# Spatial products over four banks, weights in another order, and a third adaLN chunk on VectorE

## The chip, the cores and the metric

The kernel runs on one core of a Trainium2 chip. The metric is the device time of one execution in microseconds (us). A core has TensorE (PE; its weight loads are listed apart as PEld), VectorE (DVE), ScalarE (ACT), GpSimd (POOL) and SyncE (SP), which issues the transfers here. Each takes its own instructions in order; semaphores hold them to each other. The weights and tokens lie in HBM and come through 16 DMA engines. TensorE writes to PSUM, which has eight banks of 512 fp32 values per partition.

## The reference, cut to what matters

Two layers over 512 latent and 256 context tokens of width 1024. Each layer normalises the tokens, scales and shifts them by adaLN terms (`silu(c) @ ada_w + ada_b`, split into shift, scale and gate), mixes them, and adds the gated result. Layer 0 mixes by a gated MLP (A, the place of this change) and differential attention (B); layer 1 by latent attention. Branch A:

```
u, v, z = xl @ w_in[:, :512], xl @ w_in[:, 512:1024], xl @ w_in[:, 1024:1536]
u, v = gelu(u), layer_norm(gelu(v))
mixed[p, g] = sum_q w_s[g, p, q] * v[q, g] + b_s[g, p]     # 8 groups, chunks of 128 tokens
a = u * mixed * silu(z)
```

## The kernel before

All products of fp32 operands are done in three matmuls (`mm3`, L79 to L81): each operand is split into a high part `h` (ScalarE, L66) and a low part `l` (VectorE, L67), and h·h, h·l and l·h are added up in PSUM. A weight is loaded into a `raw` buffer (two of them), split, and used.

**Order of work.** The program is traced in the order of the Python code, and a planner then sets each engine's order from priorities (the traced order), free buffers and its own estimate of times. `in_order(...)`, `issue_after(...)` and `add_manual_dep(..., NO_SYNC)` force an order on one engine where it is wanted.

**Start.** The tokens are squared and summed (`ssq_quarter` on ACT, `ssq_vector` on DVE), `rstd_of` (L266 on) gives 1/rms of the four latent tiles, and later of the two context tiles; `normalise` (L395) scales the tokens, PE turns them (`turned`, L402), and `modulate_in` (L405 on) makes the high part on ACT (L414) and, on DVE, `xm` (L416) and the low part (L421). All this stands within `in_order(ACT, DVE, PE)` for the first quarter of the width (L455 on).

**The gated MLP** (L542 to L574) comes after the products of v (`av_part`), whose layer norm runs on DVE and ACT meanwhile.
- Two projections for u (`b` = 0, 1), each of three pairs of token tiles, 48 matmuls of 256 columns a pair (`proj_tok`). When a pair is done, `ev` takes it out with a Gelu (L548).
- Eight spatial groups (L557 on): three matmuls of 384 columns into a bank of `ps_mm`, which has two, and one DVE instruction (L563) that adds the bias and multiplies by u.
- Two projections for z, taken out with a Silu (L568) into `z` (two buffers) and multiplied in on DVE (L572).

**adaLN chunks.** What the two layers need of `silu(c) @ ada_w` is cut into 12 chunks. Chunks go two ways. On PE (`ada_step`, called from `ev`): four transfers of 512 KB, then `ada_products` (L175), one copy, and in the next `ev` a transpose (`ada_rows`, L188). On DVE (`ada_piece`): a chunk is four pieces; a piece is one transfer of 512 KB (L236) and two multiplications with a running sum (L246), one for the latent and one for the context vector. Four chunks go over PE here (`ada_rest`), the layer 1 chunks 2 and 3 over DVE, as eight pieces. Both share the seven buffers `ada`; `pieces_ahead(n)` asks for the next n loads. The first piece may run once the layer norm is done (`normed`), the rest after the last spatial instruction.

**Queues around it.** All loads are on SP's queue, in the order that the planner gives them; a load that waits for a buffer holds up the loads behind it. The spatial weights `wsT` go into the shared pool `wp`, the weights of the z projections into the eight buffers `wo` (four weights with two parts each).

Of the kernel before, what the change touches and what calls it, by code (L numbers as in the profile page):

```python
# [18 lines left out]
P = 128  # L19
# [11 lines left out]
def tile_backbone(ctx: ExitStack, tc: tile.TileContext, a: dict, out: bass.AP):  # L31
# [71 lines left out]
    def fill(pl, tag, n):  # L103
        pl.tile([P, n], F32, tag=tag, name=tag)

    gsum = cst.tile([P, 8], F32, name="gsum")
    asum = cst.tile([P, 2, 4, 2], F32, name="asum")
    fill(cst, "fill0", 72)
    ident = cst.tile([P, P], F32, name="ident")
    cvec = const("cvec", [P, 8, 2])  # L110
    fill(cst, "fill1", 64)
# [55 lines left out]
    def shift_of(li, kt, v):  # L167
        return AD[:, li, kt // 2, kt % 2, v:v + 1]
# [37 lines left out]
        ada_rows(li, j, ada_products(ws, between))  # L206


    ada_rest = [(0, 4), (0, 5), (1, 0), (1, 1)]
    ada_loaded = []  # L210

    def ada_ahead():
# [26 lines left out]
    def ada_piece(after):  # L239

        k = len(pieces_done)
        w = pieces[k]
        j, b = divmod(k, 4)
        for v in range(2):
            jk = w if v else til(p_a, [P, D], F32, "lnwb")
            i = DVE.scalar_tensor_tensor(jk, w, 1.0, csb[v], op0=ALU.mult, op1=ALU.mult, accum_out=asum[:, j, b, v:v + 1])  # L246
            tc.add_manual_dep(i.ins, after.ins.name, NO_SYNC, reason="in_order")
        pieces_done.append(k)
        if b == 3:
            ada_bias(1, 2 + j, asum[:, j])  # L250

    def gate_rows(g, li, v):

# [148 lines left out]
            PE.transpose(ps[:, t * P:(t + 1) * P], xq[j][:, t0 + t, i * P:(i + 1) * P], ident)  # L402
        return ps[:, :n * P]

    def modulate_in(j, v, i, xh, xl, ps=None, between=None):  # L405

        t0, n = ((0, 4), (4, 2))[v]
        cols = slice(t0 * P, (t0 + n) * P)
        kt = 2 * j + i
        if ps is None:  # L410
            ps = turned(j, v, i, tr_ps())
        m = til(p_in, [P, NL], F32, "xm", 2)[:, :n * P]
        g = gT[:, 0, kt, v:v + 1]
        h = ACT.activation(xh[:, i, cols], ps, AF.Identity, bias=shift_of(0, kt, v), scale=g)  # L414
        if v == 0:
            DVE.tensor_scalar(m, ps, g, shift_of(0, kt, v), op0=ALU.mult, op1=ALU.add)  # L416
        else:
            ACT.activation(m, ps, AF.Identity, bias=shift_of(0, kt, v), scale=g)
        if between:
            between()  # L420
        DVE.tensor_tensor(xl[:, i, cols], m, xh[:, i, cols].bitcast(F32), op=ALU.subtract)  # L421
        return h


# [37 lines left out]
    with in_order(ACT, DVE, PE):  # L462
        normalise(0, 0)
        xt0 = []

        def fill_in(kt):
            if kt < 5:
                turn_over(2)
            else:
                i = len(xt0)  # L470
                xt0.append(turned(0, 0, i, tr_ps() if i else avb[4]))
        ada_chunk(0, 0, adaw[0], between=fill_in)
        ACT.activation(w0h, w0, AF.Copy)
        turn_over(6)
        modulate_in(0, 0, 0, *XT[0], ps=xt0[0],
                    between=lambda: DVE.tensor_tensor(w0l, w0, w0h.bitcast(F32), op=ALU.subtract))
        for q in range(1, 4):
            ssq_vector(q, 5)
        modulate_in(0, 0, 1, *XT[0], ps=xt0[1])
        for q in range(4):  # L480
            ssq_quarter(xq[q], acc, q, 4, 1 if q else 2)
        rs.append(rstd_of(acc, 4, 2))
        normalise(1, 0)
        h = normalise(0, 1)
    ws_in = [(w0h, w0l)]
# [57 lines left out]
    ada_ahead()  # L543

    au = [til(p_mix, [P, 6, 256], F32, "au", 2) for _ in range(2)]
    for b in range(2):
        def ev(p, ps, b=b):
            ACT.activation(au[b][:, 2 * p:2 * p + 2, :], ps, AF.Gelu)  # L548
            if b and p == 1:
                ada_piece(normed)  # L550
            ada_step()
            if b:
                pieces_ahead((4, 2, 2)[p])
        proj_tok(XT, load_w256(wch[4 + 2 * b:6 + 2 * b], *((p_a, 8) if b else ())), range(3), ev)

    wsh, wsl = (x.rearrange("p (g n) -> p g n", g=8) for x in load_w(a["wsT"]))
    for g in range(8):  # L557
        ps = mm_ps()
        o = ps[:, :384].rearrange("p (t n) -> p t n", t=6)
        s = (slice(None), slice(None), slice(g * 64, (g + 1) * 64))  # L560
        mm3(o, (wsh[:, g, :], wsl[:, g, :]), (vnh[s], vnl[s]), True, True)
        u = au[g // 4][:, :, (g % 4) * 64:(g % 4 + 1) * 64]
        last = [DVE.scalar_tensor_tensor(u, o, absT[:, g:g + 1], u, op0=ALU.add, op1=ALU.mult)]  # L563

    for b in range(2):
        def ev(p, ps, b=b):
            z = sp.tile([P, 2, 256], F32, tag="z", name=nm("z"))
            ACT.activation(z, ps, AF.Silu)  # L568
            ada_step()
            for _ in range(1 if b + p else 2):  # L570
                ada_piece(last[-1])
            i = DVE.tensor_tensor(au[b][:, 2 * p:2 * p + 2, :], au[b][:, 2 * p:2 * p + 2, :], z, op=ALU.mult)  # L572
            last.append(i)
        proj_tok(XT, load_w256(wch[8 + 2 * b:10 + 2 * b], p_a, 8), range(3), ev)  # L574


    p_a.release()
# [451 lines left out]
    silu2(csl, load_raw(a["crow"][0]))  # L1029

    def gate_step(b, after):
        w = load_raw(a["adr"][8 + b])
        i = DVE.scalar_tensor_tensor(w, w, 0.5, csl, op0=ALU.mult, op1=ALU.mult, accum_out=gsum[:, b:b + 1])
        tc.add_manual_dep(i.ins, after.name, NO_SYNC, reason="in_order")
        if b == 7:
            DVE.tensor_tensor(AD[:, 1, 4:, :, 0], gsum.rearrange("p (j b) -> p j b", j=2), adab[:, 1, 4:, :], op=ALU.add)
# [99 lines left out]
def _layout(i):  # L1136
    A = {k: np.asarray(v) for k, v in i.items()}
    r = {}
    x = np.concatenate([A["x"][0], A["ctx"][0]], 0)
    r["x"] = x.reshape(6, P, 4, 256).transpose(2, 1, 0, 3)  # L1140
    c = np.stack([A["c"][0], A["c_ctx"]], 0)
    r["cvec"] = c.reshape(2, 8, P).transpose(2, 1, 0)
    r["normw"] = A["norm_w"].reshape(2, 8, P).transpose(2, 0, 1)
    ada, adab = [], []
    for li in range(2):
        W = A["ada_w"][li].T
        for j in range(6):
            if j < 4:
                rows = np.r_[j * 256:(j + 1) * 256, D + j * 256:D + (j + 1) * 256]
            else:  # L1150
                rows = np.arange(2 * D + (j - 4) * 512, 2 * D + (j - 3) * 512)
            ada.append(W[rows].reshape(4, P, D))
            adab.append(A["ada_b"][li][rows])
    r["ada"] = np.stack([w.reshape(512, 4, 2, P).transpose(1, 3, 2, 0).reshape(4, P, 1024) for w in ada])
    r["adr"] = np.concatenate(ada[8:12])
    r["crow"] = np.broadcast_to(c[:, None], (2, P, D))
    r["adab"] = np.stack(adab).reshape(2, 6, 4, P).transpose(3, 0, 1, 2)
    r["cos"], r["sin"] = _rope_tables()
    r["absT"] = A["a_bs"][0].T
    r["subw"] = A["b_subln_w"][0][:, None]  # L1160
    lqk = np.stack([A["b_lq1"][0], A["b_lk1"][0], A["b_lq2"][0], A["b_lk2"][0]])
    r["lqk"] = np.broadcast_to(lqk, (P, 4, 64))
    r["lnwb"] = np.broadcast_to(np.stack([A["a_ln_w"][0], A["a_ln_b"][0]]), (P, 2, 512))
    w = A["even_w_in"][0]
    au, av, az = w[:, :512], w[:, 512:1024], w[:, 1024:1536]
    bq, bk, bv, bz = w[:, 1536:2048], w[:, 2048:2560], w[:, 2560:3072], w[:, 3072:]
    qk = np.stack([_chunks(bq, 128, 8), _chunks(bk, 128, 8)], 1).reshape(8, P, 1024)
    r["ew"] = np.concatenate([_chunks(av, 512, 2), _chunks(au, 256, 4), _chunks(az, 256, 4), _chunks(bv, 256, 4),
                              qk, _chunks(bz, 128, 8)])
    r["wsT"] = A["a_ws"][0].transpose(2, 0, 1).reshape(P, 1024)  # L1170
    r["ewo"] = _chunks(A["even_w_out"][0], 256, 4)
    o = A["odd_w_in"][0]
    owa = o[:, :448].reshape(8, P, 448).transpose(1, 0, 2)
    r["owa"] = owa.reshape(P, 4, 896).transpose(1, 0, 2)
    r["owz"] = _chunks(o[:, 448:], 128, 8)
    wq = A["c_wq_b"][0].reshape(256, 8, 192)
    r["wqT"] = wq[:, :, :128].transpose(2, 1, 0).reshape(P, 2, 1024).transpose(1, 0, 2)
    r["wqr"] = wq[:, :, 128:].reshape(2, P, 512).transpose(1, 0, 2).reshape(P, 1024)
    wkv = A["c_wkv_b"][0].reshape(128, 8, 256)
    r["wkT"] = wkv[:, :, :128].transpose(2, 1, 0).reshape(P, 1024)  # L1180
    r["wv"] = wkv[:, :, 128:].reshape(P, 1024)
    r["cqw"] = A["c_q_norm_w"][0].reshape(2, P).T
    r["ckw"] = A["c_kv_norm_w"][0][:, None]
    r["owo"] = _chunks(A["odd_w_out"][0], 256, 4)
    r["finw"] = np.broadcast_to(A["final_w"], (P, D))
    return {k: np.ascontiguousarray(v, dtype=np.float32) for k, v in r.items()}
# [14 lines left out]
```

## Time and profile before

| | |
|---|---|
| median of 3 runs | 697.11 us (697.02 to 700.86) |
| profiled execution | 698.24 us; its span 696.5 us, so 1.7 us lie around the span |
| granted clock over the span | 0.996 |
| busy share of the span | PE 98%, PEld 90%, DVE 67%, ACT 52%, POOL 3% |
| chain that ended last | PE 77%, DVE 4%, ACT 2%, DMA 1% |

A busy PE says that matmuls are in flight, not that they follow each other at full pace; so the starts of the matmuls are read too. A row of a timeline gives start, duration, engine, line, operation, output and inputs, shape, how many were merged, and in brackets the idle time of the engine before it and what ended it.

### The profile page before, as it was taken

Reading aid. Unit: us, or ns where it says so; the run is one execution under the profiler, and the core shown is the slowest. Engines: PE = TensorE matmul, PEld = TensorE weight load, DVE = VectorE, ACT = ScalarE, POOL = GpSimd, SP = SyncE. Lnnn points to the kernel's source line nnn. Section 1 sums busy time; section 2 is a strip of 40 time slices with the busy share of each in tenths; the row PEclk is TensorE's granted clock in tenths of the full one; section 3 lists DMA queues with packets and bytes.
Section 4 is the critical chain, followed back from the end, with each engine's and each line's share of the span. In section 5 each row is a group of like instructions: output and inputs, shape, how many; then the busy total and the mean of one; then the engine's idle time right before and its main releaser. Section 6 shows DMA issues by size and latency. Waiting matters only on the chain.

```text
span 696.5 us, 12408 instructions
## 1 busy us (share of the span) xinstructions
PE 682.5 (98%) x5118; PEld 628.9 (90%) x5118; DVE 468.5 (67%) x867; ACT 364.5 (52%) x706; POOL 20.3 (3%) x27
## 2 busy tenths in 40 slices
PE   8999998999999999999999999999999999999995
PEld 8678997999998899899899999988889999999995
DVE  2647738646597965979675428766458898876764
ACT  5856324115475754766534314444358787886432
POOL 1000000010001000010000000010000000000000
PEclk9999999999999999999999999999999999999998
DMA  8965894101100011000613300250210212110402
GB/s 339 408 230 224 310 372 155 31 1 61 62 31 31 1 61 61 32 30 1 242 61 119 111 1 10 65 198 31 92 61 9 83 62 62 32 61 31 121 32 92
DMA packets 20361, 69.93 MB, mean 100 GB/s; under 512 B 3152, under 2 KB 3280, under 8 KB 20304
## 3 DMA queue, kind: packets, MB, share of 16 engines
q1 hardware_dynamic: 20304, 69.13, 28.2%
q8 instruction: 40, 0.66, 0.4%
q14 instruction: 17, 0.14, 0.1%
HBM read 67.02 MB, written 2.10 MB: 99 GB/s over the span
## 4 chain that ended last, share of the span: by engine, by line
PE 77%; DVE 4%; ACT 2%; DMA 1%; issue 0%; SPq 0%; POOLq 0%; ACTq 0%
PE mm L79 17%; PE mm L81 17%; PE mm L80 17%; PE S L80 3%; PE S L81 3%; PE S L79 3%; PE tr L1005 3%; PE S L644 2%; PE S L646 2%; PE tr L662 2%; PE S L983 1%; PE S L987 1%; DMA wr<-in_ew 1%; PE tr L79 1%; PE tr L679 1%; PE tr L293 1%
## 5 line engine op out<-in xcount | busy, mean ns | idle before, releaser
L80 PE MATMUL mm<-xl,wh 128*128 128x512 f32 (+1 forms) x240 | 84.6, 352 | 0.0
L81 PE MATMUL mm<-xh,wl 128*128 128x512 f32 (+1 forms) x240 | 84.5, 352 | 0.0
L79 PE MATMUL mm<-xh,wh 128*128 128x512 f32 (+1 forms) x240 | 84.2, 351 | 0.0
L67 DVE TENSOR_TENSOR wl<-wr,wh 128x1024 fp32r<-128x1024 f32 (+1 forms) x40 | 48.3, 1209 | 41.2 <-ACT wh L66 39.6
L369 ACT ACTIVATE e<-S,s 128x768 f32<-128x768 f32 (+1 forms) x80 | 65.3, 817 | 17.4 <-DVE s L368 16.7
L368 DVE TENSOR_REDUCE s<-S 128x1 f32<-128x768 f32 (+1 forms) x80 | 67.2, 842 | 3.7 <-PE S L987 1.8
L66 ACT ACTIVATE wh<-wr 128x1024 fp32r<-128x1024 f32 (+1 forms) x40 | 41.8, 1048 | 50.9 <-PE mm L80 21.3
L66 ACT ACTIVATE ah<-tr 128x512 fp32r<-128x512 f32 x76 | 43.9, 596 | 24.8 <-PE tr L662 12.6
L67 DVE TENSOR_TENSOR al<-tr,ah 128x512 fp32r<-128x512 f32 x76 | 50.3, 685 | 7.6 <-ACT ah L66 6.7
L79 PEld LDWEIGHTS mm<-xh,wh 128*128 128x128 f32 x240 | 45.2, 188 | 5.1 <-ACT wh L66 0.2
L79 PE MATMUL mm<-wh,xh 128*128 128x256 f32 (+1 forms) x172 | 49.7, 289 | 0.0
L80 PEld LDWEIGHTS mm<-xl,wh 128*128 128x128 f32 x240 | 45.1, 188 | 5.0
L80 PE MATMUL mm<-wl,xh 128*128 128x256 f32 (+1 forms) x172 | 49.6, 288 | 0.0
L81 PEld LDWEIGHTS mm<-xh,wl 128*128 128x128 f32 x240 | 45.2, 188 | 4.8
L81 PE MATMUL mm<-wh,xl 128*128 128x256 f32 (+1 forms) x172 | 49.0, 287 | 0.0
L79 PE MATMUL mm<-wo,xh 128*128 128x256 f32 x144 | 40.7, 283 | 0.9 <-DVE au L563 0.9
L81 PE MATMUL mm<-wo,xl 128*128 128x256 f32 x144 | 40.3, 280 | 0.0
L80 PE MATMUL mm<-wo,xh 128*128 128x256 f32 x144 | 40.3, 280 | 0.0
L79 PEld LDWEIGHTS mm<-wh,xh 128*128 128x128 f32 x172 | 32.5, 189 | 1.1 <-ACT xh L414 0.3
L156 POOL TENSOR_TENSOR s<-s,mhalf 128x6 f32<-128x6 f32 (+4 forms) x15 | 16.0, 1071 | 585.6 <-DVE s L1107 225.1
L80 PEld LDWEIGHTS mm<-wl,xh 128*128 128x128 f32 x172 | 32.4, 188 | 0.4
L81 PEld LDWEIGHTS mm<-wh,xl 128*128 128x128 f32 x172 | 32.3, 188 | 0.5
(330 smaller groups left out, 2000.6 us busy)
## 6 DMA issues: line engine op xcount, KB each, us to landing
ada<-in_ada SPq DMA_DIRECT2D x32, 512.0 KB, 7.8
wr<-in_ew SPq DMA_DIRECT2D x28, 512.0 KB, 3.5
ada<-in_adr SPq DMA_DIRECT2D x8, 512.0 KB, 6.6
wr<-in_ewo SPq DMA_DIRECT2D x8, 512.0 KB, 3.4
wr<-in_owz SPq DMA_DIRECT2D x8, 512.0 KB, 3.6
wr<-in_adr SPq DMA_DIRECT2D x8, 512.0 KB, 3.4
wr<-in_owo SPq DMA_DIRECT2D x8, 512.0 KB, 3.9
xr<-in_x SPq DMA_DIRECT2D x4, 768.0 KB, 6.3
```

The source lines that it names most:

```text
L66: ACT.activation(h, src, AF.Copy)
L67: (eng or DVE).tensor_tensor(l, src, h.bitcast(F32), op=ALU.subtract)
L79: PE.matmul(ps, lh, rh, start=first, stop=False)
L80: PE.matmul(ps, lh, rl, start=False, stop=False)
L81: PE.matmul(ps, ll, rh, start=False, stop=last)
L156: return POOL.tensor_tensor(dst, src, mhalf[:, :n], op=ALU.pow)
L368: mx = DVE.tensor_reduce(nmx[:, :1], v[:, :, :w], axis=AX.XY, op=ALU.max, negate=True)
L369: ACT.activation(e.rearrange("p (c k) -> p c k", k=w), v[:, :, :w], AF.Exp, bias=nmx[:, :1], scale=1.0, accum_out=sm[:, col:col + 1])
L644: PE.matmul(S[:, c, :n], QS[:, m, qs], KS[:, m, k0:k0 + n], start=True, stop=False)
L646: scored = PE.matmul(S[:, c, :n], QS[:, m, qs], KL[:, m, k0:k0 + n], start=False, stop=True)
L662: PE.transpose(ps[:, i * 256 + q * P:i * 256 + (q + 1) * P], es[q][:, (2 * j + i) * P:(2 * j + i + 1) * P], ident)
L1005: PE.transpose(ps[:, i * 256 + q * P:i * 256 + (q + 1) * P], es[q][:, (2 * j + i) * P:(2 * j + i + 1) * P], ident)
```

## The change

- The spatial products go by turns into `ps_mm` and into the first half of a tile of `ps_s`: four banks rather than two.
- Chunk (1, 1) leaves `ada_rest` and becomes four more pieces on DVE; the running sums are one chunk larger, the layout of the piece weights starts one chunk earlier. Pieces are spread anew: 2 before the spatial instructions (1 before), then 2, 2, 2, 2, 1, 1 over the six pairs of the z projections (2, 1, 1, 1, 1, 1 before). Loads of pieces are asked for from the last pair of the first u projection on.
- Weights: `wsT` and those of the first z projection are traced ahead of the second u projection; those of the second z projection keep their place, but their ACT part is put behind the last Gelu, their DVE part behind the last spatial instruction.
- At the start, `xm` and the low part of the second turned tile come after `rstd_of` of the context tiles on DVE, instead of before.

```
-    asum = cst.tile([P, 2, 4, 2], F32, name="asum")
-    fill(cst, "fill0", 72)
+    asum = cst.tile([P, 3, 4, 2], F32, name="asum")
+    fill(cst, "fill0", 64)
...
-    ada_rest = [(0, 4), (0, 5), (1, 0), (1, 1)]
+    ada_rest = [(0, 4), (0, 5), (1, 0)]
...
-            ada_bias(1, 2 + j, asum[:, j])
+            ada_bias(1, 1 + j, asum[:, j])
...
-    def modulate_in(j, v, i, xh, xl, ps=None, between=None):
+    def modulate_in(j, v, i, xh, xl, ps=None, between=None, only=None):
...
         h = ACT.activation(xh[:, i, cols], ps, AF.Identity, bias=shift_of(0, kt, v), scale=g)
-        if v == 0:
-            DVE.tensor_scalar(m, ps, g, shift_of(0, kt, v), op0=ALU.mult, op1=ALU.add)
-        else:
-            ACT.activation(m, ps, AF.Identity, bias=shift_of(0, kt, v), scale=g)
-        if between:
-            between()
-        DVE.tensor_tensor(xl[:, i, cols], m, xh[:, i, cols].bitcast(F32), op=ALU.subtract)
+
+        def low():
+            if v == 0:
+                DVE.tensor_scalar(m, ps, g, shift_of(0, kt, v), op0=ALU.mult, op1=ALU.add)
+            else:
+                ACT.activation(m, ps, AF.Identity, bias=shift_of(0, kt, v), scale=g)
+            if between:
+                between()
+            DVE.tensor_tensor(xl[:, i, cols], m, xh[:, i, cols].bitcast(F32), op=ALU.subtract)
+        if only == "h":
+            return low
+        low()
         return h
...
-        modulate_in(0, 0, 1, *XT[0], ps=xt0[1])
+        second = modulate_in(0, 0, 1, *XT[0], ps=xt0[1], only="h")
         for q in range(4):
             ssq_quarter(xq[q], acc, q, 4, 1 if q else 2)
         rs.append(rstd_of(acc, 4, 2))
+        second()
         normalise(1, 0)
...
+    w_az, behind = [], {}
     for b in range(2):
         def ev(p, ps, b=b):
-            ACT.activation(au[b][:, 2 * p:2 * p + 2, :], ps, AF.Gelu)
-            if b and p == 1:
+            gelu = ACT.activation(au[b][:, 2 * p:2 * p + 2, :], ps, AF.Gelu)
+            behind[ACT.engine] = gelu.ins.name
+            if b and p < 2:
                 ada_piece(normed)
             ada_step()
-            if b:
-                pieces_ahead((4, 2, 2)[p])
-        proj_tok(XT, load_w256(wch[4 + 2 * b:6 + 2 * b], *((p_a, 8) if b else ())), range(3), ev)
-
-    wsh, wsl = (x.rearrange("p (g n) -> p g n", g=8) for x in load_w(a["wsT"]))
+            if b or p == 2:
+                pieces_ahead((4, 3, 2, 3)[3 * b + p - 2])
+        w = load_w256(wch[4 + 2 * b:6 + 2 * b], *((p_a, 8) if b else ()))
+        if b:
+            wsh, wsl = (x.rearrange("p (g n) -> p g n", g=8) for x in load_w(a["wsT"]))
+            w_az.append(load_w256(wch[8:10], p_a, 8))
+        proj_tok(XT, w, range(3), ev)
+
     for g in range(8):
-        ps = mm_ps()
+        ps = ps_s.tile([P, 2, 512], F32, tag="S", name=nm("S"))[:, 0, :] if g % 2 else mm_ps()
...
+    behind[DVE.engine] = last[-1].ins.name
     for b in range(2):
         def ev(p, ps, b=b):
...
             ada_step()
-            for _ in range(1 if b + p else 2):
+            for _ in range(2 if 3 * b + p < 4 else 1):
                 ada_piece(last[-1])
...
-        proj_tok(XT, load_w256(wch[8 + 2 * b:10 + 2 * b], p_a, 8), range(3), ev)
+        if b:
+
+            n = len(nc.cur_bb.bb.instructions)
+            w_az.append(load_w256(wch[10:12], p_a, 8))
+            for i in nc.cur_bb.bb.instructions[n:]:
+                if i.engine in behind:
+                    tc.add_manual_dep(i, behind[i.engine], NO_SYNC, reason="in_order")
+        proj_tok(XT, w_az[b], range(3), ev)
...
-        w = load_raw(a["adr"][8 + b])
+        w = load_raw(a["adr"][12 + b])
...
-    r["adr"] = np.concatenate(ada[8:12])
+    r["adr"] = np.concatenate(ada[7:12])
```

## Rows read from the trace of the kernel before

**Rows 1.** The page, engines: busy us, share of the span, instructions.
```profile
PE 682.5 (98%) x5118; PEld 628.9 (90%) x5118; DVE 468.5 (67%) x867; ACT 364.5 (52%) x706; POOL 20.3 (3%) x27
```
**Rows 2.** Windows: length, then busy us (instructions) by engine, granted clock, DMA share, GB/s.
```profile
105.00:115.00 10.00, 7.28 (x41) 5.54 (x41) 7.58 (x11) 4.17 (x5) 0.00 (x0) 1.00 0.44 141
115.00:130.00 15.00, 15.00 (x129) 15.00 (x129) 13.41 (x23) 3.97 (x5) 0.00 (x0) 1.00 0.32 107
130.00:150.00 20.00, 20.00 (x167) 19.78 (x167) 10.18 (x21) 2.39 (x4) 2.94 (x4) 1.00 0.00 1
```
**Rows 3.** Timeline of PE over the spatial products (L79 to L81).
```profile
106.60 0.34 PE L79 MATMUL mm<-vnh,wh 128*128 128x384 f32 x1
...
106.95 0.33 PE L81 MATMUL mm<-vnh,wl 128*128 128x384 f32 x1
107.56 0.44 PE L79 MATMUL mm<-vnh,wh 128*128 128x384 f32 x1 [0.28 <-ACT au L548]
...
108.87 0.44 PE L79 MATMUL mm<-vnh,wh 128*128 128x384 f32 x1 [0.52 <-DVE au L563]
...
111.05 0.45 PE L79 MATMUL mm<-vnh,wh 128*128 128x384 f32 x1 [0.86 <-DVE au L563]
...
112.56 0.44 PE L79 MATMUL mm<-vnh,wh 128*128 128x384 f32 x1 [0.19 <-DVE au L563]
...
114.75 0.39 PE L79 MATMUL mm<-wo,xh 128*128 128x256 f32 x1 [0.87 <-DVE au L563]
```
**Rows 4.** Timeline of DVE over the same stretch.
```profile
107.06 1.23 DVE L67 TENSOR_TENSOR wo<-wr,wo 128x1024 fp32r<-128x1024 f32 x1 [5.49 <-ACT wo L66]
108.20 1.14 DVE L563 SCALAR_TENSOR_TENSOR au<-mm,absT_sb,au 128x384 f32<-128x384 f32 x2
109.25 1.22 DVE L67 TENSOR_TENSOR wo<-wr,wo 128x1024 fp32r<-128x1024 f32 x1
...
112.94 1.22 DVE L67 TENSOR_TENSOR wl<-wr,wh 128x1024 fp32r<-128x1024 f32 x1
114.08 1.14 DVE L563 SCALAR_TENSOR_TENSOR au<-mm,absT_sb,au 128x384 f32<-128x384 f32 x2
```
**Rows 5.** Timeline of ACT at the end of the u projections.
```profile
105.97 1.06 ACT L66 ACTIVATE wo<-wr 128x1024 fp32r<-128x1024 f32 x1 [4.33 <-DMA wr<-in_ew]
106.93 0.58 ACT L548 ACTIVATE au<-mm 128x512 f32<-128x512 f32 x1
```
**Rows 6.** Timeline of PE around the fourth chunk (L175) and the transpose after it (L188).
```profile
93.18 0.27 PE L188 MATMUL tr<-ident,arow 128*128 128x128 f32 x1
93.39 1.96 PE L175 MATMUL tr<-ada,c 128*32 128x128 f32 x64
95.27 0.38 PE L79 MATMUL mm<-wo,xh 128*128 128x256 f32 x1
...
100.84 0.27 PE L188 MATMUL tr<-ident,arow 128*128 128x128 f32 x1
```
**Rows 7.** Timeline of ACT, one Silu of the z projections.
```profile
132.02 0.60 ACT L568 ACTIVATE z<-mm 128x512 f32<-128x512 f32 x1 [5.05 <-PE mm L81]
```
**Rows 8.** Timeline of all engines at the start, around the context tiles' 1/rms.
```profile
20.61 0.81 DVE L416 TENSOR_SCALAR xm<-tr,gT,AD 128x512 f32<-128x512 f32 x1
...
22.06 0.15 DVE L268 TENSOR_REDUCE s<-s 128x2 f32<-128x8 f32 x1
...
22.20 0.30 PEld L457 LDWEIGHTS mm<-wh,xl 128*128 128x128 f32 x2 [0.46 <-DVE xl L421]
...
23.80 0.84 PE L402 MATMUL tr<-ident,x 128*128 128x128 f32 x4 [0.40 <-ACT x L395]
...
25.18 0.50 PE L79 MATMUL S<-wh,xh 128*128 128x512 f32 x1 [0.55 <-ACT xh L414]
```
**Rows 9.** Groups by line up to 260 us: xcount, busy us, mean ns, idle before.
```profile
L246 DVE SCALAR_TENSOR_TENSOR lnwb<-ada,ob 128x1024 f32<-128x1024 f32 x8 | 9.8, 1220 | 0.5 <-DMA ada<-in_adr 0.5
```
**Rows 10.** Timeline of SP's queue, loads of pieces.
```profile
94.09 3.19 SPq L236 DMA_DIRECT2D ada<-in_adr  x5
```

## The prediction

> **What bounds the kernel.** First the page's engines: PE is busy for 682.5 of 696.5 us, the others far less [rows 1]. So time comes off in two ways only: fewer matmuls, or closing a place where PE waits. Then the windows: PE is full in the z projections, and in one window of this part it is busy for 7.28 of 10 us [rows 2]. PE's timeline shows why: from the first spatial matmul at 106.60 to the first z matmul at 114.75, 8.15 us, it stops five times, once for the Gelu, four times for a DVE addition that has to free a bank [rows 3]. DVE's timeline shows what kept the additions: three weight splits of 1.14 to 1.2 us each stand between them [rows 4]. The Gelu itself stood behind a split on ACT, at 106.93 instead of at once [rows 5]. The granted clock is 1.00 there, the upper level of 2.4 GHz [rows 2], so the loss is waiting and no slower clock.
>
> **The change, part by part.**
>
> *The chunk off PE.* A block of 48 matmuls with a chunk in front goes from one transpose to the next, 93.18 to 100.84: 7.66 us [rows 6]. A block without a chunk takes 5.05 + 0.60 = 5.65 us from Silu to Silu [rows 7]. The difference, 2.01 us, is what one chunk with its transpose costs on PE. I take 2.0. Bounds: the chunk's own stretch is 93.39 to 95.27, 1.9; with the transpose, from 93.18, 2.1 [rows 6]. Its copy on ACT goes too, at nothing: ACT waits there.
>
> *The spatial products.* One group's matmuls start at 106.60 and the third at 106.95, so a group is 0.35 + 0.17 = 0.52 us [rows 3], eight are 4.2. An addition takes 1.14 / 2 = 0.57 us [rows 4]. With four banks PE needs for group 4 the bank of group 0: PE is there after 2.1 us, the addition is done after 0.52 + 0.2 + 0.57 = 1.3 (0.2 us for handing over and back, an estimate from the 0.1 us between the first of the last two additions, done at 114.08 + 0.57, and PE's start at 114.75 [rows 3, 4]). The margin of 0.8 us shrinks by 0.05 a group, so it lasts for eight. The Gelu's bank is now wanted by group 2, after 1.05 us, when a Gelu of 0.58 [rows 5] that nothing holds is done. So the stage goes from 8.15 to some 4.3: 3.85 us. This rests on DVE doing only additions there. The three splits leave: two belong to the second z projection and are now forced behind the last addition; the third is of a later weight, and its `raw` buffer is now taken until those two are split. Pieces 0 and 1 hang on the layer norm alone, and are asked for a block earlier. Upper bound 3.95, no wait at all; lower bound 1.6: two instructions of 1.2 us [rows 9] still fall between the additions.
>
> *The start.* Moving `xm` and the low part behind `rstd_of` lets the reduce start at 20.7 instead of 22.06: 1.4 us earlier [rows 8]. The low part, which PE waits for at 22.20, comes 0.4 later (reduce and scaling, 0.2 each). PE then ends the passes at about 23.6 and finds the normalised context tiles ready, where it waited until 23.80. The four transposes no longer pause, and the matmul at 25.18, which waits for ACT [rows 8], starts some 0.4 us earlier: I take 0.4. Bounds: nothing, if ACT's order makes it late as before; 0.7, if the wait of 0.55 goes whole and the transposes close up.
>
> *More on DVE.* In the two windows of the z projections DVE is busy for 13.41 + 10.18 = 23.6 us of 35 [rows 2]. To it come six piece instructions (20 instead of 14), the two splits put behind the additions and the third one: nine of 1.14 us, 10.3. That is 33.9 us, just what six blocks of 5.65 take [rows 7]. So DVE becomes full there, but PE needs little of it: a block's multiplication frees a `z` buffer that is wanted two blocks later, 11.3 us on. A backlog of up to 4 us (two pieces, 4.9 us, before a multiplication [rows 9]) is hidden; the last two blocks hold one piece each and let DVE catch up. I cost it at nothing; without that cover it costs what DVE runs late for the next weights (first rival).
>
> Here a page speaks against the change. A piece reads two fp32 tensors from SBUF and sums: 1220 ns for 1024 columns [rows 9], as long as a split of the same shape that sums nothing, 1.22 to 1.23 us [rows 4]. The Trainium skill, "Vector Engine (DVE) Microarchitecture Reference", section "Points that are easy to get wrong", says that such an instruction with two non-bf16 SBUF sources runs at half throughput. The trace does not show it against the split; were a piece instruction 2.4 us, 20 of them would be 49 us, and DVE would end the z projections some 24 us late.
>
> *The weights.* SP's queue has the same bytes: four transfers of a chunk become four of pieces, asked for later. `wsT` and the first z weights are traced earlier; PE does not wait for weights in [rows 3], so I cost that at nothing. The second z weights are split later; they are wanted three blocks, 17 us, after the additions end, and need 2 × 1.2 us of DVE and a load that can be done before. The layer 1 gate pieces change only their place in HBM: nothing.
>
> **The sum.** 2.0 + 3.85 + 0.4 = 6.25 us off the profiled execution's 698.2 us (span 696.5 and 1.7 around it), so 692.0. The median of the runs is 697.1, 1.1 lower, and by the same sum **690.9 us**. PE is full behind this part [rows 1], so what is won there arrives at the end. Its own range is 689.6 to 692.2.
>
> **Rivals.**
>
> 1. *DVE is full and the next weights are late.* The planner puts the split for the q projection, lowest in priority, behind the last pieces. Of the 33.9 us no slack is left, so it would be 1 to 2.5 us late. For: the sum above. Against: the two light last blocks. Price 2.5: 693.4. Chance 0.17.
> 2. *The additions stay mixed.* Pieces 0 and 1, held by a late transfer, fall between the additions; a piece waited 0.5 us for its transfer before [rows 9], and five loads stood 3.19 us on SP [rows 10]. Price 1.2 to 2.3: 692.1 to 693.2. Chance 0.1.
> 3. *Slower: the second z weights come late.* Pieces 9 to 11 need buffers that pieces 2 to 4 free only after the additions. If their loads stand ahead of the weights on SP's in-order queue, as five loads of pieces stood ahead of the weights that arrive at 105.97 [rows 10, 5], the weights land some 12 us after the additions, and the two splits then queue behind pieces, 4.9 us each block [rows 9]. PE would wait up to 8 us: 6.25 − 8 is 1.7 us slower, 698.8. It decides from the point where the second split ends more than 6 us after PE wants it. Against: those weights need none of the pieces' buffers, so a planner that passes over what lacks a buffer can put them first; no row settles it. Chance 0.05.
> 4. *The page's rule holds for the added pieces.* 24 us: 709. Chance 0.01, since all eight of one kind took 1220 ns on average [rows 9].
> 5. *The change does more.* A block after a chunk has 48 matmuls in 100.84 − 95.27 = 5.57 us [rows 6], restart and all, one without 5.65 [rows 7]. Should the z blocks take that pace, six give 0.5 more; with the start's 0.7 and no wait at all, 689.9. Chance 0.12.
>
> The forecast keeps 0.55.
>
> **How the numbers follow.** 8 in 10: from 689.3, a little under rival 5, to 694.4, a little over rival 1; outside are rivals 3 and 4 and the tails. A measurement of this kernel can tell about 1% from no change, and 1% is 7 us: 690.1 or less counts as faster. There lie the lower part of the forecast's own range (0.16) and most of rival 5 (0.1): 0.26. Slower by 1%, over 704, are rival 4 and a worse rival 3: 0.03. Within 1%: 0.71.
>
> **What would show it.** Right: L175 has 64 records less, and L246 eight more; the stretch from the first spatial matmul to the first z matmul is 4.2 to 4.5 us, with no idle time ended by DVE; no L67 and no L246 stands between the L563; L268 comes before the second L416, and the first matmul behind the context transposes starts near 24.8; the z blocks are 5.65 us apart, DVE nearly full beside them. Wrong: idle time of PE in front of the fourth z block or of the q projection, ended by DVE or a transfer (rivals 3, 1); L246 among the L563 (rival 2); a total gain that doesn't sit in these three places, which would say that the planner moved something further on.

## The result, and the profile after

The changed kernel takes **691.9 us** (median, 690.97 to 692.24) beside 697.2 us for the kernel before in the same measurement: ratio 0.9906, interval 0.9883 to 0.9928. The forecast said 690.9 in a range of 689.3 to 694.4; 691.9 lies in it and in the forecast's own narrower range. The profiled execution took 691.32 us, its span 689.4.

The page of the changed kernel, engines (busy us, share of the span, instructions) and the first line of the chain that ended last:

```profile
PE 679.4 (99%) x5053; PEld 628.9 (91%) x5053; DVE 477.2 (69%) x883; ACT 363.5 (53%) x705; POOL 20.3 (3%) x27
...
PE 91%; DVE 4%; ACT 3%; issue 0%; POOL 0%; POOLq 0%; ACTq 0%; DVEq 0%
```

65 PE instructions are gone (64 of a chunk and its transpose), VectorE has 16 more (eight multiplications and the read-out of each one's sum), and of the chain of waits PE now holds 91% where it held 77%. Its timeline over the spatial products (L79 to L81; start, duration, engine, line, operation, shape, idle before in brackets), to be read against [rows 3]:

```profile
103.88 0.34 PE L79 MATMUL mm<-vnh,wh 128*128 128x384 f32 x1
...
104.40 0.33 PE L79 MATMUL S<-vnh,wh 128*128 128x384 f32 x1
...
104.92 0.33 PE L79 MATMUL mm<-vnh,wh 128*128 128x384 f32 x1
...
105.96 0.33 PE L79 MATMUL mm<-vnh,wh 128*128 128x384 f32 x1
...
108.04 0.28 PE L79 MATMUL mm<-wo,xh 128*128 128x256 f32 x1
```

No row carries a bracket: a group starts every 0.52 us, and from 103.88 to 108.04 the stage takes 4.17 us instead of 8.15. VectorE from there to the q projection (L574 is the addition, L584 the multiplication by z, L246 a piece, L67 a split):

```profile
104.60 0.62 DVE L574 SCALAR_TENSOR_TENSOR au<-mm,absT_sb,au 128x384 f32<-128x384 f32 x1 [5.90 <-PE mm L81]
...
108.33 0.61 DVE L574 SCALAR_TENSOR_TENSOR au<-S,absT_sb,au 128x384 f32<-128x384 f32 x1
108.86 1.22 DVE L246 SCALAR_TENSOR_TENSOR lnwb<-ada,ob 128x1024 f32<-128x1024 f32 x1
...
110.00 1.22 DVE L67 TENSOR_TENSOR wo<-wr,wo 128x1024 fp32r<-128x1024 f32 x1
...
113.42 1.22 DVE L67 TENSOR_TENSOR wo<-wr,wo 128x1024 fp32r<-128x1024 f32 x1
...
142.79 0.69 DVE L584 TENSOR_TENSOR au<-au,z 128x512 f32<-128x512 f32 x1 [1.25 <-ACT z L580]
148.31 0.01 DVE L347 LOAD_MASK_SELECT sh<-z  x1 [4.83 <-ACT z L624]
```

Eight additions follow each other 0.52 to 0.56 us apart with nothing between; pieces and the two splits of the second z weights come behind them. DVE is full until 141.4, and yet it then waits for ACT twice: the pieces fit. The windows of the changed kernel say the same of both engines (columns as in [rows 2]):

```profile
108.00:115.00 7.00, 7.00 (x62) 7.00 (x61) 7.00 (x11) 0.87 (x2) 0.00 (x0) 1.00 0.38 105
115.00:130.00 15.00, 15.00 (x130) 15.00 (x129) 15.00 (x27) 4.00 (x5) 0.00 (x0) 1.00 0.57 199
```

ACT's timeline: the last Gelu (L555), the splits of the second z weights now behind it, and two Silu:

```profile
104.08 0.60 ACT L555 ACTIVATE au<-mm 128x512 f32<-128x512 f32 x1 [5.06 <-PE mm L81]
104.57 2.00 ACT L66 ACTIVATE wo<-wr 128x1024 fp32r<-128x1024 f32 x2
...
136.51 0.60 ACT L580 ACTIVATE z<-mm 128x512 f32<-128x512 f32 x1 [5.05 <-PE mm L81]
142.16 0.60 ACT L580 ACTIVATE z<-mm 128x512 f32<-128x512 f32 x1 [5.06 <-PE mm L81]
```

The z blocks keep their 5.65 us. At the start, all engines' timeline of the changed kernel, against [rows 8]:

```profile
17.52 0.73 PE L462 MATMUL mm<-wh,xh 128*128 128x512 f32 x2
...
21.18 0.16 DVE L268 TENSOR_REDUCE s<-s 128x2 f32<-128x8 f32 x1
...
21.46 0.80 DVE L418 TENSOR_SCALAR xm<-tr,gT,AD 128x512 f32<-128x512 f32 x1
22.30 0.69 DVE L423 TENSOR_TENSOR xl<-xm,xh 128x512 fp32r<-128x512 f32 x1
...
22.93 0.84 PE L402 MATMUL tr<-ident,x 128*128 128x128 f32 x4 [0.37 <-ACT x L395]
23.52 0.71 PE L462 MATMUL mm<-wh,xl 128*128 128x512 f32 x2
...
24.55 0.40 PE L79 MATMUL S<-wh,xh 128*128 128x512 f32 x1
```

Where the 7.1 us of the two profiled spans come from, by marks in both traces:

| mark | before | after | gained up to here | in this step |
|---|---|---|---|---|
| first matmul with the tokens (L457, now L462) | 17.13 | 17.52 | −0.39 | −0.39 |
| first Gelu of u | 70.53 | 69.81 | 0.72 | 1.11 |
| first spatial matmul | 106.60 | 103.88 | 2.73 | 2.01 |
| first z matmul | 114.75 | 108.04 | 6.70 | 3.98 |
| last Silu of z | 148.98 | 142.16 | 6.82 | 0.1 |
| end of the span | 696.5 | 689.4 | 7.1 | 0.3 |

So the steps at the three places of the prediction hold 7.10 us; the first matmul, 0.39 later, takes that much back, and 0.4 more comes behind them. The medians differ by 5.3 us, not by 6.9 as the profiled executions do: the profiled one of before lay 1.0 above its median, that of after 0.6 below. Three later measurements, on other occasions and three chips, gave the kernel before medians of 698.4 to 698.9; so the gain may be nearer 7 us than 5.3, but the changed kernel ran only once beside them (690.73 us). Part of such a spread is there before PE has begun on the tokens: the mark of the table's first row lies between 17.06 and 18.22 in the fourteen traces.

### The profile page after: what moved, and what is told of

It is laid out like the page before. It is cut to its first block, busy times and chain, and to the rows that moved or that the text cites. A ratio compares the mean times of both kernels' runs of the same rounds, so it can differ in the third digit from the quotient of the medians.

```text
span 689.4 us, 12288 instructions
## 1 busy us (share of the span) xinstructions
PE 679.4 (99%) x5053; PEld 628.9 (91%) x5053; DVE 477.2 (69%) x883; ACT 363.5 (53%) x705; POOL 20.3 (3%) x27
## 4 chain that ended last, share of the span: by engine, by line
PE 91%; DVE 4%; ACT 3%; issue 0%; POOL 0%; POOLq 0%; ACTq 0%; DVEq 0%
PE mm L79 19%; PE mm L81 19%; PE mm L80 19%; PE S L79 5%; PE S L80 5%; PE S L81 5%; PE tr L1024 3%; PE S L663 2%; PE S L665 2%; PE tr L175 2%; PE tr L681 2%; PE S L446 2%; PE S L1002 1%; PE S L1006 1%; PE tr L698 1%; PE tr L293 1%
## 5 line engine op out<-in xcount | busy, mean ns | idle before, releaser
L81 PE MATMUL mm<-xh,wl 128*128 128x512 f32 (+1 forms) x240 | 84.5, 352 | 0.0
L79 PE MATMUL mm<-xh,wh 128*128 128x512 f32 (+1 forms) x240 | 84.1, 351 | 0.0
L67 DVE TENSOR_TENSOR wl<-wr,wh 128x1024 fp32r<-128x1024 f32 (+1 forms) x40 | 48.3, 1210 | 38.3 <-ACT wh L66 36.8
L67 DVE TENSOR_TENSOR al<-tr,ah 128x512 fp32r<-128x512 f32 x76 | 50.4, 685 | 7.6 <-ACT ah L66 6.7
L79 PEld LDWEIGHTS mm<-xh,wh 128*128 128x128 f32 x240 | 45.2, 188 | 5.2 <-ACT wh L66 0.2
L79 PE MATMUL mm<-wh,xh 128*128 128x256 f32 (+1 forms) x172 | 49.8, 289 | 0.0
L81 PEld LDWEIGHTS mm<-xh,wl 128*128 128x128 f32 x240 | 45.1, 188 | 4.6 <-DVE wl L67 0.2
L81 PE MATMUL mm<-wh,xl 128*128 128x256 f32 (+1 forms) x172 | 49.3, 287 | 0.0
L79 PE MATMUL mm<-wo,xh 128*128 128x256 f32 x144 | 40.6, 282 | 0.0
L81 PE MATMUL mm<-wo,xl 128*128 128x256 f32 x144 | 40.4, 281 | 0.0
L79 PEld LDWEIGHTS mm<-wh,xh 128*128 128x128 f32 x172 | 32.5, 189 | 0.8 <-issue 0.4
L81 PEld LDWEIGHTS mm<-wh,xl 128*128 128x128 f32 x172 | 32.4, 189 | 0.5
```

Source lines behind the costliest of these rows:

```text
L67: (eng or DVE).tensor_tensor(l, src, h.bitcast(F32), op=ALU.subtract)
L79: PE.matmul(ps, lh, rh, start=first, stop=False)
L81: PE.matmul(ps, ll, rh, start=False, stop=last)
```

## The experiments

Ten kernels, and two kernels once more (after_again is the changed kernel, banks_again is banks_alone), each beside the kernel before on its chip (before's medians: 698.4 in the first group, 698.9 in the second, 698.5 in the third).

| kernel | median us | ratio, interval | spatial stage us | z block us |
|---|---|---|---|---|
| banks_alone | 694.95 | 0.9950 [0.9934, 0.9965] | 5.11 | 5.44 |
| order_alone | 696.2 | 0.9966 [0.9951, 0.9981] | 6.01 | 5.65 |
| chunk_alone | 698.61 | 1.0009 [0.9996, 1.0023] | 13.0 | 5.65 |
| start_alone | 696.85 | 0.9981 [0.9971, 0.9992] | 7.95 | 5.44 |
| after_two_banks | 691.85 | 0.9907 [0.9888, 0.9926] | 6.00 | 5.44 |
| after_no_behind | 692.4 | 0.9903 [0.9886, 0.9921] | 4.85 | 5.65 |
| four_chunks | 688.87 | 0.9857 [0.9837, 0.9876] | 4.17 | 5.65 |
| pieces_all_late | 691.08 | 0.9890 [0.9873, 0.9908] | 4.17 | 5.65 |
| chunk_and_order | 694.15 | 0.9935 [0.9917, 0.9953] | 5.98 | 5.44 |
| chunk_late_loads | 696.19 | 0.9965 [0.9950, 0.9980] | 7.90 | 5.44 |
| after_again | 690.73 (one execution) | | 4.17 | 5.65 |
| banks_again | 693.98 (one execution) | | 4.38 | 5.44 |

A caution for the times: a z block lasts 5.44 or 5.65 us by a pace whose cause was not found (last section). Over six blocks that is 1.3 us, and only the profiled execution of a kernel shows which pace it had. So what a part is worth is read from the stages; a median alone does not show it.

### The four parts, each alone

**Four banks**, in the kernel before:

```
-        ps = mm_ps()
+        ps = ps_s.tile([P, 2, 512], F32, tag="S", name=nm("S"))[:, 0, :] if g % 2 else mm_ps()
```

> The kernel before with the spatial products over four banks and nothing else of the change. Theory (PE waits for the bank; with four it runs ahead of VectorE, so a split in front of the additions costs it little): the stretch from the first spatial to the first z matmul falls from 8.15 to 4.3 to 4.7 us, the time by 3.5 us to some 693.7. Rival (what costs is the splits on VectorE, the number of banks doesn't matter): 696 or more.

DVE's timeline in that kernel:

```profile
107.70 1.23 DVE L67 TENSOR_TENSOR wo<-wr,wo 128x1024 fp32r<-128x1024 f32 x1 [6.11 <-ACT wo L66]
108.84 0.61 DVE L563 SCALAR_TENSOR_TENSOR au<-mm,absT_sb,au 128x384 f32<-128x384 f32 x1
...
112.52 0.61 DVE L563 SCALAR_TENSOR_TENSOR au<-S,absT_sb,au 128x384 f32<-128x384 f32 x1
```

One split remains ahead of the additions and none between them, though nothing in this kernel's text forbids it. The likely reason, which no run tests: with PE no longer held up, the planner had no hole to fill. The stage falls by 3.04 us to 5.11 in this trace, not to the expected 4.3 to 4.7. What is left over 4.17 is mostly the Gelu, which here stands behind a split on ACT (the third group comes 0.54 us late), and then the first addition, late behind its own split (groups 0.63 to 0.68 us apart); in banks_again, where the stage began 0.7 us later, the Gelu was in time and the stage took 4.38. So the three splits between the additions [rows 4] look like a consequence of the two banks as much as a cause of the delay. The median is 3.5 us lower, as expected, but this trace has the faster z pace, 1.3 us of it.

**The new order of weights**, two banks kept (`wsT` and the first z weights ahead of the second u projection; the second z weights behind the last Gelu and the last spatial instruction, as in the change):

```
+        if b:
+            wsh, wsl = (x.rearrange("p (g n) -> p g n", g=8) for x in load_w(a["wsT"]))
+            w_az.append(load_w256(wch[8:10], p_a, 8))
...
+                    tc.add_manual_dep(i, behind[i.engine], NO_SYNC, reason="in_order")
```

> The kernel before with the weights traced in the new order and the second z weights behind the last Gelu and the last addition, two banks. Theory: the additions follow each other, but two banks make PE wait for each addition and the hand-over; the stretch is 5.6 to 6.0 us, the time falls by 2.1 to 2.5 us to some 694.9. Rival (only the splits cost): the stretch is 4.3, the time 693.3.

The stage takes 6.01 us with nothing but additions on DVE: that is what two banks alone cost, 1.84 us over four. The order alone is worth 2.14 us there. With the 3.04 of the banks that would be 5.2; together the two give 3.98, since each removes the same splits from between the additions.

**The chunk**, in the kernel before, with the pieces spread as in the change:

```
...
-    ada_rest = [(0, 4), (0, 5), (1, 0), (1, 1)]
+    ada_rest = [(0, 4), (0, 5), (1, 0)]
...
-            if b:
-                pieces_ahead((4, 2, 2)[p])
+            if b or p == 2:
+                pieces_ahead((4, 3, 2, 3)[3 * b + p - 2])
...
```

> The kernel before with the third chunk as pieces on VectorE, spread as in the changed kernel, two banks, old order of weights. Theory (a chunk is 2.0 us of PE and VectorE hides its pieces): 695.2, the stretch of the spatial products about 8 us as before. Rival (the pieces hold up the additions or the next weights): 697.2 or more.

It gains nothing, against the expectation. PE's timeline of that kernel, then ACT's, SP's queue, and the windows:

```profile
105.06 0.34 PE L79 MATMUL mm<-vnh,wh 128*128 128x384 f32 x1
...
109.34 0.69 PE L79 MATMUL mm<-vnh,wh 128*128 128x384 f32 x1 [3.59 <-ACT au L548]
...
118.06 0.58 PE L79 MATMUL mm<-wo,xh 128*128 128x256 f32 x1 [0.33 <-DVE au L563]
```

```profile
101.85 1.06 ACT L66 ACTIVATE wo<-wr 128x1024 fp32r<-128x1024 f32 x1 [7.41 <-DMA wr<-in_ew]
102.81 0.58 ACT L548 ACTIVATE au<-mm 128x512 f32<-128x512 f32 x1
...
107.75 1.06 ACT L66 ACTIVATE wo<-wr 128x1024 fp32r<-128x1024 f32 x1 [3.40 <-DMA wr<-in_ew]
108.71 0.58 ACT L548 ACTIVATE au<-mm 128x512 f32<-128x512 f32 x1
```

```profile
89.16 3.22 SPq L236 DMA_DIRECT2D ada<-in_adr  x6
92.47 1.66 SPq L126 DMA_DIRECT2D wr<-in_ew  x2
```

```profile
105.00:110.00 5.00, 1.41 (x7) 1.09 (x7) 1.76 (x3) 1.54 (x2) 0.00 (x0) 0.89 0.64 209
110.00:115.00 5.00, 4.54 (x14) 3.54 (x13) 3.72 (x7) 2.11 (x2) 0.00 (x0) 0.50 0.57 173
115.00:120.00 5.00, 4.67 (x21) 3.76 (x20) 4.66 (x8) 1.06 (x1) 0.00 (x0) 0.59 0.39 122
120.00:130.00 10.00, 10.00 (x87) 10.00 (x87) 9.86 (x18) 2.94 (x3) 0.00 (x0) 1.00 0.70 225
```

Read them from the last row of ACT backwards: the Gelu that PE waits for stands behind a split, the split waits for its weight, and all loads of the z weights were issued behind six loads of pieces. (The load of this one went out at 104.19, when an earlier of these weights, which had landed at 101.82 behind the pieces, gave its `raw` buffer back.) PE does reach the stage earlier, at 105.06, but then stands idle for 3.59 us. The granted clock then is 0.50, the lower level of 1.2 GHz, until about 119 (0.59 over the window from 115 to 120): a spatial matmul takes 0.52 us, and 0.69 behind a wait, instead of 0.34 and 0.44. The stage lasts 13.0 us. This profiled execution, 701.17 us, is near the slow end of the kernel's own 697.1 to 701.2; what the median shows is that the 2.0 us are lost. The fall of the clock is not this one execution's alone: the mean granted clock of the twelve runs is 0.990 to 0.997, median 0.993, where the kernel before beside them has 0.994 to 0.998, median 0.997.

**The start:**

```
-        modulate_in(0, 0, 1, *XT[0], ps=xt0[1])
+        second = modulate_in(0, 0, 1, *XT[0], ps=xt0[1], only="h")
...
+        second()
...
```

> The kernel before with the second low part behind the context tiles' 1/rms at the start, nothing else. Theory: the planner puts the context transposes ahead of the last two passes, PE no longer waits for ACT; 0.7 us (as the two profiles show at the first Gelu), so 696.5; 1.1 if the later start of the first matmul in the profile after was chance. Rival (what is won is given back at the next weights): 697.2.

From the first matmul with the tokens to the matmul behind the context transposes the move gains 1.03 us (24.61 − 17.59, against 25.18 − 17.13 in the trace before). At the first Gelu it is 1.32 (52.08 us against 53.40), at the first spatial matmul only 0.55. The two later figures hold the pace of the matmuls, too: the u block before the first Gelu ran at the faster pace here, the four with a chunk behind it at the slower, each 0.2 us. The 1.56 us by the medians stand beside z blocks of 5.44 us, 1.3 us of pace, and so are no measure of the move. Two transposes with one chunk's block between them, of which more below:

```profile
85.06 0.27 PE L188 MATMUL tr<-ident,arow 128*128 128x128 f32 x1
92.90 0.27 PE L188 MATMUL tr<-ident,arow 128*128 128x128 f32 x1
```

### What takes the banks or the forced order out of the whole

**after_two_banks** takes the line of the banks back; **after_no_behind** takes the forced places of the second z weights out:

```
-                if i.engine in behind:
+                if False:
```

> The changed kernel with the spatial products back in two banks. Theory: the stretch is 5.6 to 6.0 us instead of 4.2, idle time of PE ended by the additions comes back; 1.5 us of the gain is lost, 5.0 kept against the kernel before (693.4 where the changed kernel has 691.9). Rival (the order of the weights does it all): no loss, 691.9.

> The changed kernel without the forced order of the second z weights' splits. Theory: with four banks a split ahead of the additions costs PE little; 691.9 to 692.5. Rival (it is the forced order that frees the additions): 693.5 or more.

PE with two banks, and DVE without the forced places:

```profile
106.26 0.45 PE L79 MATMUL mm<-vnh,wh 128*128 128x384 f32 x1 [0.17 <-DVE au L574]
107.77 0.44 PE L79 MATMUL mm<-vnh,wh 128*128 128x384 f32 x1 [0.18 <-DVE au L574]
```

```profile
104.39 1.23 DVE L67 TENSOR_TENSOR wo<-wr,wo 128x1024 fp32r<-128x1024 f32 x1 [6.24 <-ACT wo L66]
105.53 0.61 DVE L574 SCALAR_TENSOR_TENSOR au<-mm,absT_sb,au 128x384 f32<-128x384 f32 x1
```

Two banks lose 1.83 us in the stage, as expected; but the time (691.85, ratio 0.9907) is the rival's, as if nothing were lost. In the trace the z blocks behind the stage last 5.44 us instead of 5.65, and the last Silu of z starts at 142.84, 0.7 us after that of the changed kernel; by the end of the span, 689.25 us, that is made up too. So what four banks are worth in the whole change rests on the stage; the time does not show it, and one trace per kernel cannot say whether the pace made it up in every run. Without the forced places one split comes ahead of the additions and costs 0.68 us of the stage, too little to be seen in the time (692.4, ratio 0.9903).

### VectorE's room

**pieces_all_late** runs no piece ahead of the spatial instructions and two in each of the six z blocks; **four_chunks** puts one more chunk, (1, 0), on VectorE: 16 pieces, six of them ahead of the spatial instructions.

```
...
-    ada_rest = [(0, 4), (0, 5), (1, 0)]
+    ada_rest = [(0, 4), (0, 5)]
...
-            if b and p < 2:
-                ada_piece(normed)
+            if b:
+                ada_piece(normed)
+                ada_piece(normed)
...
```

> The changed kernel with all twelve pieces after the spatial products, two in each of the six z pairs: 4.6 us more VectorE work where it is full. Theory (PE needs nothing of VectorE there that is urgent; its backlog ends in the 4.8 us that it is idle after the last multiplication): 691.9, no change. Rival 1 of the prediction (the next weights or the last multiplication come late): 694 to 695.

> The changed kernel with a fourth chunk, (1, 0), on VectorE: 16 pieces, six of them before the spatial products (two in each pair of the second u projection), ten after as now. Theory (a chunk is 2.0 us of PE; VectorE has some 10 us free beside the second u projection): 689.9. Rival (VectorE or the transfers are full and the additions or z weights come late): 692 to 695, with idle time of PE ended by VectorE or a transfer.

The first costs nothing: twelve pieces fit beside the z blocks. The second is **faster than both kernels**, 688.87 us, ratio 0.9857 [0.9837, 0.9876] where the changed kernel has 0.9906 [0.9883, 0.9928]. Its timeline of PE over the spatial products:

```profile
101.77 0.34 PE L79 MATMUL mm<-vnh,wh 128*128 128x384 f32 x1
...
105.94 0.28 PE L79 MATMUL mm<-wo,xh 128*128 128x256 f32 x1
```

From the spatial products to the last Silu of z everything comes 2.10 us earlier than in the changed kernel. Of this 0.09 is an earlier first matmul (17.43 against 17.52), the rest, 2.0, the chunk once more; no wait of PE appears in the z blocks. At the end of the span 1.6 us are left.

### Why the chunk alone gained nothing

Two ways of mending chunk_alone. **chunk_and_order** adds the new order of weights to it (two banks, old start). **chunk_late_loads** keeps the old order, but asks for all loads of pieces behind those of the first z weights, and runs two pieces in each z block:

```
...
-            if b:
-                pieces_ahead((4, 2, 2)[p])
...
+        if not b:
+            pieces_ahead(12)
...
```

> The kernel before with the chunk on VectorE and the new order of the weights; two banks and the old start. Theory (the chunk alone lost its 2.0 us because six loads of pieces stood ahead of five loads of weights on SP, and a split that waited for one of them stood ahead of the last Gelu on ACT; the new order mends that): what the order alone gave, 2.7 us by the medians, and the chunk's 2.0 add up, some 4.5 us off, ratio 0.9935; the first spatial matmul about 2 us earlier than with the order alone, the spatial stretch 6.0 us, no idle time of PE over 0.5 us that ends with the Gelu. Rival (the chunk doesn't pay without four banks, whatever the order): no better than the order alone, ratio 0.9966.

> The kernel before with the chunk on VectorE, old order of the weights, but the loads of all twelve pieces are asked for after those of the first z weights, and the pieces run two a pair in the z projections. Theory (SP's queue made the chunk alone fail): PE waits for the Gelu under 1 us, the granted clock stays at 1.00 through the spatial products, the stretch is 7 to 8.5 us, and the chunk's 2.0 us arrive: ratio 0.997. Rival (weights can't come sooner in the old order, whatever stands ahead of them): PE idle for over 2 us again, granted clock down, ratio 1.000 or over. Second rival: the late loads make the pieces late and the next projection's weights with them, 1 to 2.5 us of PE idle behind the z blocks.

SP's queue in chunk_late_loads:

```profile
79.91 0.92 SPq L126 DMA_DIRECT2D wr<-in_ew  x1
81.29 0.80 SPq L236 DMA_DIRECT2D ada<-in_adr  x2
87.55 0.33 SPq L126 DMA_DIRECT2D wr<-in_ew  x1
87.97 3.04 SPq L236 DMA_DIRECT2D ada<-in_adr  x5
91.10 3.24 SPq L126 DMA_DIRECT2D wr<-in_ew  x2
```

The theory's numbers came, the rival's did not. With two of the weights' loads issued ahead of the five of pieces, the last Gelu starts at 105.84, PE no longer waits for it, the clock stays at 1.00, the stage lasts 7.90 us, and the ratio is 0.9965 where chunk_alone had 1.0009. The ratio holds the faster z pace, but the chunk is seen without it: from the first Gelu to the first spatial matmul it is 34.07 us against 36.07 in the kernel before, and the stage gives none of the 2.0 back. (This kernel also runs the first pieces later on VectorE; no VectorE instruction stands in the chain that chunk_alone's rows show.)

With the new order the stage lasts 5.98 us and PE waits 0.17 us for the Gelu, so there the chunk is not taken back either. By the ratios, 0.9935 against 0.9966 for the order alone, it gives 2.2 us; but the z blocks of the two traces differ by 1.3 us of pace, so that agreement with 2.0 is luck. In the traces 1.42 us of the chunk arrive between first Gelu and first spatial matmul; the other 0.6 is the slower pace of the three u blocks that still have a chunk. So the order of the queue was the cause, and in the change it is the new order of weights that lets the chunk pay. The ratios of the four parts alone, multiplied, happen to give that of the whole (0.9950 × 0.9966 × 0.9981 × 1.0009 = 0.9906); the stages show that the parts are not independent: banks and order overlap by 1.2 us, and the chunk's 2.0 come only with weights that are loaded ahead of the pieces.

## Why the prediction was right, and where not

- **The chunk, 2.0:** 2.01 between first Gelu and first spatial matmul, and 2.0 for one more in four_chunks. The number was right, in part by luck. The sum takes a block at 118 ns from matmul to matmul, [rows 7], from one at 113, [rows 6]. At one pace a chunk costs 2.2 us: 7.66 − 5.44 in the kernel before, and 7.84 − 5.65 in start_alone, where the blocks with a chunk ran at 118. The 2.0 came because the block that lost its chunk ran at 118.
- **The weights, nothing:** the step that does not hold is "PE does not wait for weights in [rows 3], so I cost that at nothing". Nothing is what they cost in the change, but for a reason that was not seen: in the old order the loads of pieces stand ahead of the weights and take back the whole 2.0 (chunk_alone, 3.59 us of waiting). The row was there: the Gelu at 106.93 stood behind a split that waited for its weight [rows 5], and PE waited 0.28 us for that Gelu [rows 3].
- **The spatial products, 3.85 (1.6 to 3.95):** 3.98. The mechanism is as told: eight additions in a row, the Gelu freed, no bracket on PE. The stage was put at 4.3 and is 4.17, that is no wait at all.
- **The start, 0.4 (0 to 0.7):** 1.02 from the first matmul to the one behind the context transposes, and 1.03 in both after_again and start_alone. (At the first Gelu it is 1.11, 0.77 and 1.32; the differences come behind the place of the change.) Of the 1.11 the profiled execution has 0.72 left, since its first matmul came 0.39 later. The term was too small because of the order: "PE then ends the passes at about 23.6 and finds the normalised context tiles ready". It doesn't; the planner puts the four transposes ahead of the last passes (22.93, then 23.52 in the rows of the start). The passes now cover both the low part and ACT's work on the turned context tiles, so the 0.46 and the 0.55 of [rows 8] go away; 0.37 of a wait for the normalising stays.
- **The sum:** 6.25 against 6.9 between the profiled executions, so 692.0 against 691.32. The three steps themselves hold 7.10, the start 0.7 more than forecast; the later first matmul brings the sum nearer, which is chance. The time put down, 690.9, was 1.0 under the median: it took off 1.1 us because the median of three runs lay under the profile. That baseline was itself uncertain by as much (697.0 to 700.9).
- **DVE full (rival 1):** full it is, 7.00 of 7 and 15.00 of 15 us, but the planner put the next splits among the pieces and not behind them (L67 at 117.60 and 124.00), and DVE is idle for 4.83 us before q's first result. **Pieces among the additions (rival 2):** pieces 0 and 1 ran from 83.88 to 88.84, long before the additions. **Second z weights late (rival 3):** their loads stand ahead of those of pieces 9 to 11 on SP, the splits end at 114.6, and PE has no idle time in front of the fourth z block. The mechanism of that rival, loads of pieces ahead of weights, is what chunk_alone shows, one projection earlier.
- **The page's rule (rival 4):** the 24 instructions of L246, by groups of the changed kernel up to 260 us (count, busy us, mean ns, idle before):

```profile
L246 DVE SCALAR_TENSOR_TENSOR ada<-ada,ob 128x1024 f32<-128x1024 f32 x12 | 14.7, 1222 | 0.1
L246 DVE SCALAR_TENSOR_TENSOR lnwb<-ada,ob 128x1024 f32<-128x1024 f32 x12 | 14.7, 1222 | 1.1 <-DMA ada<-in_adr 1.1
```

All 24 took 1218 to 1228 ns, as long as a split of that shape, 1.22 us. The Trainium skill, "Vector Engine (DVE) Microarchitecture Reference", section "Points that are easy to get wrong", speaks of half throughput for such operands; against the split it does not show in any of them. The price that the rival was given, 709, does not follow from its 24 us either: 690.9 + 24 is 715.
- **The change does more (rival 5):** the z blocks kept 5.65 us, so not by that way. The rival had seen the faster pace in the block of [rows 6]; z blocks with it do occur, but in other kernels.

## What to carry to other kernels

Before work is moved off the busy engine, follow the transfers that the move pulls forward: on an in-order queue they can push a weight, and with it whatever stands behind that weight's first instruction, into the path. In chunk_alone a stall of PE cost more than its length: 3.59 us of waiting made the stage 4.9 us longer, with the granted clock at 0.50 for some 10 us. And parts of a change that cure the same stall are not to be added up: price them by what is left when all of them are there.

## What the runs showed that was not expected

Matmuls of 256 columns that follow each other without a wait keep one of two paces, 113 or 118 ns from start to start, at a granted clock of 1.00 in both. It makes a z block 5.44 or 5.65 us, 1.3 us over six. Two Silu of the kernel with four banks alone, against 136.51 and 142.16 above:

```profile
139.14 0.60 ACT L568 ACTIVATE z<-mm 128x512 f32<-128x512 f32 x1 [4.84 <-PE mm L81]
144.58 0.60 ACT L568 ACTIVATE z<-mm 128x512 f32<-128x512 f32 x1 [4.84 <-PE mm L81]
```

Two programs were run once more, unaltered, to see whether the pace belongs to the program.

> The changed kernel once more, unaltered, for the pace of its z blocks. If the pace of 113 or 118 ns between matmuls of 256 columns belongs to the program: z blocks of 5.65 us again, and each earlier stretch at the pace that it had. If it belongs to the execution: in some stretch the other pace, in the z blocks 5.44 us and a span of some 688.1 us instead of 689.4.

> The kernel before with four banks alone once more, unaltered, for the pace. If it belongs to the program: z blocks of 5.44 us again and a span of 692.7 us. If to the execution: 5.65 us in the z blocks with some chance, and then 1.2 us more.

In the z blocks it came back as it was: 117 to 119 ns in all 287 intervals of the changed kernel, 5.44 us blocks with the banks alone. Elsewhere it did not: from 248 to 261 us the changed kernel kept 118 ns (to 1 ns) in 98 of 100 intervals the first time and 113 ns in 101 of 105 the second. So it is not fixed by the program, and in this stretch nothing in the program differs. The u blocks have both paces too: the four with a chunk in front ran at 113 ns in the kernel before and at 118 in start_alone. In many places the pace changes where other work on PE comes between two runs of such matmuls (a chunk's products, transposes), but not only there: in the kernel before it turns from 113 to 118 at 165.44 us without a pause, where weights and tokens change places as the operands of the products. What decides it was not found; it stays open, and differences of about 1 us between kernels here, those of after_two_banks among them, should not be read as the merit of an edit.
